# Moving the additive step of every RMSNorm from GpSimd to ScalarE in a one-layer hybrid decoder kernel

## The chip, the cores and the metric

The kernel runs on one core of one Trainium2 chip. The metric is the device time of one execution in microseconds (us). A core has five engines with queues of their own: TensorE (PE in the profile; its weight loads are PEld), VectorE (DVE), ScalarE (ACT), GpSimd (POOL) and SyncE (SP), which here only issues DMAs. Each queue runs in order; engines wait for one another through semaphores.

## The reference

One decoder layer over 512 tokens of 1024 channels, all in float32. The sub-layers matter here only for where the norms stand:

```
def rms_norm(x, g):
    y = x * rsqrt(mean(x * x, axis=-1) + 1e-6)
    return y * g

h = rms_norm(x, g_mix_pre);  u, q, k, v = split(h @ w_in)
y = concat[pool_mixer(u), moba_attention(q, k, v)] @ w_out
x = x + rms_norm(y, g_mix_post)
h = rms_norm(x, g_ffn_pre)
x = x + rms_norm(conv_ffn(h), g_ffn_post)
x = x + (p @ w_ple) * sigmoid(x @ w_ple_gate)
```

So there are four norms, each over 512 tokens.

## The kernel before

The 512 tokens are four tiles (t = 0 to 3) of 128 tokens, one token per partition. Every norm is done once per tile, so there are sixteen reciprocal roots, and, as one of the norms adds in two steps, twenty additions. Matmuls run in float32r; each operand is split into a high part (`h`) and a low part (`l`), and a product is three matmuls (`mm3`, L231 to L235). Weights arrive by SyncE's DMAs in two rotating `raw` buffers; ScalarE writes the high part `wh` (L146), VectorE the low part `wl` (L153), and when both halves of a chunk are split its `raw` buffer goes to the next load. How many splits run ahead is written into the program by `W.ahead(n)`; the order on each engine is the order of the code.

A norm of one tile is a chain over three engines. `mean_square` (L255) lets ScalarE square the tile and accumulate the mean square into a 128x1 column `ms`; the profile shows this as an ACTIVATE and an ACTIVATION_READ_ACCUMULATOR on L258. `rstd_of` (L261) then has GpSimd add a constant (L263) and raise to the power -0.5 (L264). VectorE multiplies the tile by the result.

- `first_norm(t)` (L341, names `msx`, `rx`, `hn`): the norm ahead of w_in. Its result is transposed on TensorE (`put_transposed`, L274) and split into `hT`; the value projections `v` stand between the tiles.
- The norm after w_out is over two halves of 512 channels that are finished at different times. The first half's mean square gets the constant at L635 on GpSimd (`s`, four columns); `second_norm(t)` (L641) takes the second half's mean square, and there `rstd_of` adds the column `s` in place of the constant (`ry`). VectorE updates the residual `x` (L646), and the norm ahead of the FFN follows at once (`msh`, `rh`, `h2n`, L649 to L653), then the transposes of that tile.
- `third_norm(t)` (L841, `msd`, `rd`): the norm after the FFN.

Of the kernel before, what the change touches and what calls it, by code (L numbers as in the profile page):

```python
# [17 lines left out]
F32 = mybir.dt.float32  # L18
F32R = mybir.dt.float32r
AF = mybir.ActivationFunctionType  # L20
ALU = mybir.AluOpType
# [3 lines left out]
P = 128  # L25
# [9 lines left out]
EPS = 1e-6  # L35
# [137 lines left out]
def hybrid_layer(ctx, tc, x, p, rel_bias, g_mix_pre, g_mix_post, g_ffn_pre, g_ffn_post, w_in, w_pool,  # L173
                 pool_scale, w_out, w_up, conv_w, conv_b, w_down, w_ple, w_ple_gate, onehot, out):
    nc = tc.nc
    act, dve, pool, pe, sp = nc.scalar, nc.vector, nc.gpsimd, nc.tensor, nc.sync

    const = ctx.enter_context(tc.tile_pool(name="const", bufs=1))
# [67 lines left out]
    pscale = cols[:, 4 * NF:]  # L246
    mhalf = const.tile([P, 1], F32, name="mhalf")
    pool.memset(mhalf, -0.5)

    def gains(pl, g, name):  # L250
        t = pl.tile([P, D], F32, name=name)
        pool.dma_start(t, bass.AP(tensor=g.tensor, offset=g.offset, ap=[[0, P], [1, D]]))
        return t

    def mean_square(src, junk, name):  # L255

        ms = small.tile([P, 1], F32, tag="ms", name=name)
        act.activation(junk, src, AF.Square, scale=D ** -0.5, accum_out=ms)  # L258
        return ms

    def rstd_of(ms, name, add=EPS):  # L261
        r = small.tile([P, 1], F32, tag="rstd", name=name)
        pool.tensor_scalar(r, ms, add, None, op0=ALU.add)  # L263
        pool.tensor_tensor(out=r, in0=r, in1=mhalf, op=ALU.pow)  # L264
        return r

# [74 lines left out]
    def first_norm(t):  # L341
        hn[t] = early.tile([P, D], F32, tag="hn", name=f"hn{t}", bufs=2)
        r = rstd_of(mean_square(xs[t], hn[t], f"msx{t}"), f"rx{t}")
        for c in range(2):
            part = slice(c * 512, (c + 1) * 512)
            dve.scalar_tensor_tensor(hn[t][:, part], xs[t][:, part], r, g_ps[c], op0=ALU.mult, op1=ALU.mult)
# [243 lines left out]
    def out_part(t, n, ks, first, last):  # L590
        if first:
            yb[t, n] = bank(f"y{t}_{n}", "mm" if t < 2 else "s")
        token_product(yb[t, n], t, wo, ks, first, last, y_stationary)
# [33 lines left out]
    for t in range(NT):  # L627
        out_part(t, 0, (3,) if t < 2 else (2, 7, 3), False, True)
        if t == NT - 1:
            wo = [W.take() for _ in range(4)]  # L630
            W.ahead(1)
        junk = op_.tile([P, D], F32, tag="hn", name=f"junk{t}", bufs=2)
        ms = mean_square(yb[t, 0], junk[:, :512], f"msy{t}_0")
        s = op_.tile([P, 1], F32, tag="s0", name=f"s0_{t}", bufs=NT)
        pool.tensor_scalar(s, ms, EPS, None, op0=ALU.add)  # L635
        s0.append(s)
        dve.tensor_mul(ya[t][:, :512], yb[t, 0], g_post[:, :512])
        if t < NT - 1:
            W.ahead(2)

    def second_norm(t, n=0):  # L641
        hn = op_.tile([P, D], F32, tag="hn", name=f"h2n{t}", bufs=2)
        ms = mean_square(yb[t, 1], hn[:, :512], f"msy{t}_1")
        dve.tensor_mul(ya[t][:, 512:], yb[t, 1], g_post[:, 512:])
        r = rstd_of(ms, f"ry{t}", s0[t])
        dve.scalar_tensor_tensor(X[t], ya[t], r, X[t], op0=ALU.mult, op1=ALU.add)  # L646
        if t:
            put_transposed(t - 1, h2[t - 1], "pt")
        ms = mean_square(X[t], hn, f"msh{t}")  # L649
        dve.tensor_mul(ya[t], X[t], g_pre)  # L650
        r = rstd_of(ms, f"rh{t}")
        W.ahead(n)
        dve.tensor_scalar_mul(hn, ya[t], r)  # L653
        h2.append(hn)
# [455 lines left out]
```

## Time and profile before

| | us |
|---|---|
| median of 3 runs | 592.13 (590.53 to 592.85) |
| the profiled execution | 590.47 |
| its span, first to last instruction | 588.6 |
| TensorE busy in the span | 580.1 |
| VectorE busy | 429.9 |
| ScalarE busy | 294.4 |
| GpSimd busy | 233.4 |

The busy times overlap, since the engines run side by side. The profiled execution lasts 1.87 us longer than its span, and it is a little faster than the fastest of the three timed runs. TensorE ran at its upper clock level nearly throughout: the mean granted clock is 0.998.

### The profile page before, as it was taken

The page shows a single profiled execution, that of the slowest core. Times are in us where ns is not written, and L with a number is a line of the kernel's source. Part 1 is how long each engine was busy: PE and PEld are TensorE (multiplying, and loading weights), DVE is VectorE, ACT ScalarE, POOL GpSimd, SP SyncE. Part 2 cuts the span into 40 slices and gives each one's busy share as a digit, 9 for nine tenths or more (in the row PEclk, how much of TensorE's full clock was granted, in tenths as well). Part 3 has the DMA queues.
Part 4 walks back from the last instruction along what each step waited for, and adds up shares of the span by engine and source line. Part 5 has one row for each costly group of instructions (what it writes and reads, how often), then busy time and mean ns, then how long its engine had stood idle before and what let it go on. Part 6 is the DMA issues. An engine that isn't in the chain of part 4 may idle for free.

```text
span 588.6 us, 7522 instructions
## 1 busy us (share of the span) xinstructions
PE 580.1 (99%) x2765; PEld 484.8 (82%) x2765; DVE 429.9 (73%) x560; ACT 294.4 (50%) x478; POOL 233.4 (40%) x236
## 2 busy tenths in 40 slices
PE   8999999999999999999999999999999999999996
PEld 6788888888879988888888888888888888888885
DVE  5625786888488668697854667967777785879985
ACT  6524665665455424334432434535465665757561
POOL 2200230066035389999604696574210000003920
PEclk9999999999999999999999999999999999999999
DMA  8779833624640988999935566858364575768563
GB/s 293 207 250 293 225 102 90 171 82 177 221 139 0 338 306 272 361 338 362 330 122 168 190 215 218 296 200 286 142 205 153 198 286 179 267 199 307 188 222 139
DMA packets 70237, 128.58 MB, mean 218 GB/s; under 512 B 4163, under 2 KB 37791, under 8 KB 68792
## 3 DMA queue, kind: packets, MB, share of 16 engines
q1 hardware_dynamic: 60472, 88.56, 46.9%
q0 software_dynamic: 9584, 39.41, 18.2%
q8 instruction: 22, 0.36, 0.2%
q10 hardware_dynamic: 144, 0.13, 0.1%
q14 instruction: 15, 0.12, 0.1%
HBM read 97.65 MB, written 26.76 MB: 211 GB/s over the span
## 4 chain that ended last, share of the span: by engine, by line
PE 91%; DMA 3%; DVE 2%; ACT 2%; issue 1%; SPq 1%; POOL 0%; DVEq 0%; ACTq 0%; POOLq 0%
PE gate L233 6%; PE valu L233 6%; PE gate L234 6%; PE valu L235 6%; PE gate L235 6%; PE valu L234 6%; PE d L233 6%; PE d L235 6%; PE d L234 6%; PE g L233 2%; PE g L235 2%; PE g L234 2%; PE s L464 2%; PE o L513 2%; DMA xa<-in_x 2%; PE pt L493 1%
## 5 line engine op out<-in xcount | busy, mean ns | idle before, releaser
L153 DVE TENSOR_TENSOR wl<-raw,wh 128x1024 fp32r<-128x1024 f32 (+1 forms) x118 | 161.7, 1378 | 25.5 <-ACT wh L146 25.2
L146 ACT CAST wh<-raw 128x1024 fp32r<-128x1024 f32 (+1 forms) x118 | 119.0, 1024 | 28.7 <-DMA raw<-in_w_up 13.2
L769 POOL TENSOR_TENSOR b<-b 128x512 f32<-128x512 f32 x60 | 96.6, 1621 | 12.1 <-DMA b<-in_w_down 9.6
L233 PE MATMUL gate<-hT,wl 128*128 128x512 f32 x160 | 62.3, 389 | 0.0
L234 PE MATMUL gate<-hT,wh 128*128 128x512 f32 x160 | 62.3, 389 | 0.0
L234 PE MATMUL valu<-hT,wh 128*128 128x512 f32 x160 | 62.2, 389 | 0.0
L235 PE MATMUL valu<-hT,wh 128*128 128x512 f32 x160 | 62.2, 389 | 0.0
L235 PE MATMUL gate<-hT,wh 128*128 128x512 f32 x160 | 62.2, 389 | 0.0
L233 PE MATMUL valu<-hT,wl 128*128 128x512 f32 x160 | 62.2, 389 | 0.0
L233 PE MATMUL d<-wh,ml 128*128 128x512 f32 x154 | 60.0, 390 | 0.1
L235 PE MATMUL d<-wh,mh 128*128 128x512 f32 x154 | 59.9, 389 | 0.0
L234 PE MATMUL d<-wl,mh 128*128 128x512 f32 x154 | 59.9, 389 | 0.0
L263 POOL TENSOR_SCALAR rd<-msd 128x1 f32<-128x1 f32 x4 | 1.7, 422 | 108.3 <-ACT M L258 108.3
L713 ACT ACTIVATE sq<-sq 128x512 f32<-128x512 f32 x22 | 13.9, 632 | 53.4 <-DVE sq L712 53.4
L701 ACT ACTIVATE c<-gate,cols 128x512 f32<-128x512 f32 x20 | 15.4, 772 | 48.4 <-PE gate L235 48.4
L534 POOL TENSOR_TENSOR u<-u 128x512 f32<-128x512 f32 x10 | 10.6, 1063 | 72.1 <-ACT u L530 71.6
L235 PEld LDWEIGHTS gate<-hT,wh 128*128 128x128 f32 x160 | 30.0, 188 | 6.3
L235 PEld LDWEIGHTS valu<-hT,wh 128*128 128x128 f32 x160 | 30.0, 188 | 6.3
L234 PEld LDWEIGHTS valu<-hT,wh 128*128 128x128 f32 x160 | 30.0, 188 | 6.2
L233 PEld LDWEIGHTS valu<-hT,wl 128*128 128x128 f32 x160 | 30.0, 188 | 6.2
L233 PEld LDWEIGHTS gate<-hT,wl 128*128 128x128 f32 x160 | 30.0, 188 | 6.2
L234 PEld LDWEIGHTS gate<-hT,wh 128*128 128x128 f32 x160 | 30.0, 188 | 6.2
(252 smaller groups left out, 1334.5 us busy)
## 6 DMA issues: line engine op xcount, KB each, us to landing
raw<-in_w_up SPq DMA_DIRECT2D x22, 1024.0 KB, 5.9
b<-in_w_down POOLq DMA_DIRECT2D x22, 512.0 KB, 7.1
tsum<-b POOLq DMA_DIRECT2D x11, 1024.0 KB, 5.4
raw<-tsum SPq DMA_DIRECT2D x20, 512.0 KB, 4.3
raw<-in_w_down SPq DMA_DIRECT2D x15, 512.0 KB, 4.5
raw<-in_w_in SPq DMA_DIRECT2D x12, 512.0 KB, 6.4
k<-qk SPq DMA_DIRECT2D x16, 256.0 KB, 4.8
raw<-in_w_out SPq DMA_DIRECT2D x4, 1024.0 KB, 5.3
```

The source lines that it names most:

```text
L146: self.nc.scalar.copy(pair[0], view)
L153: self.nc.vector.tensor_sub(pair[1], view, pair[0].bitcast(F32))
L233: pe.matmul(o, st[1], mv[0], start=first, stop=False, skip_group_check=more)
L234: pe.matmul(o, st[0], mv[1], start=False, stop=False, skip_group_check=more)
L235: pe.matmul(o, st[0], mv[0], start=False, stop=last, skip_group_check=more)
L464: pe.matmul(bk[b][:, c:c + n], q[:, i * P:n], k[:, a, :n], start=a == 1, stop=a == 0)
L493: pe.transpose(ps[:, c * P:(c + 1) * P], L[h][:, o:o + P], ident)
L513: pe.matmul(o, w, moving(PT[c], j), start=j == 0 and c == 0, stop=j == NT - 1 and c == 1)
L534: pool.tensor_tensor(out=nxt[:, 16:], in0=src[:, 16:], in1=src[:, 16 - (1 << lvl):16 + S - (1 << lvl)], op=ALU.add)
L701: act.activation(c0, pg, AF.Identity, bias=cw[:, 3, f:f + 1], scale=cw[:, 2, f:f + 1])
L713: act.activation(sq, sq, AF.Tanh, scale=GELU_A * GELU_C)
L769: pool.tensor_tensor(out=b[:, o, :], in0=b[:, i0, :], in1=b[:, i1, :], op=ALU.subtract)
```

## The change

All additions of the norms go from GpSimd to ScalarE. A column `eps` of 128x1 is filled once at the start; an Identity activation with a bias column adds it, or the column `s`, to the mean square. The power stays on GpSimd.

```
+    eps = const.tile([P, 1], F32, name="eps")
+    pool.memset(eps, EPS)
...
     def rstd_of(ms, name, add=EPS):
         r = small.tile([P, 1], F32, tag="rstd", name=name)
-        pool.tensor_scalar(r, ms, add, None, op0=ALU.add)
+        act.activation(r, ms, AF.Identity, bias=eps if add is EPS else add)
         pool.tensor_tensor(out=r, in0=r, in1=mhalf, op=ALU.pow)
         return r
...
         s = op_.tile([P, 1], F32, tag="s0", name=f"s0_{t}", bufs=NT)
-        pool.tensor_scalar(s, ms, EPS, None, op0=ALU.add)
+        act.activation(s, ms, AF.Identity, bias=eps)
         s0.append(s)
```

TensorE, VectorE and SyncE keep their order. ScalarE's queue gets 20 instructions, each right behind the squares it belongs to; the two table loads in it stay two. GpSimd's loses 20 and gets the one that fills `eps`.

ScalarE's queue from the last tile's first half (`msy3_0`) to the second tile's second half (`msy1_1`), before:

```order
L258 ACTIVATE junk3_1573,msy3_0_1574<-y3_0_1444 128x512
L238 CAST pT0_1487<-trp0_1604 128x512
L238 CAST pT0_1487<-trp1_1611 128x512
L146 CAST wh25_1618<-raw12_1524 128x1024
L258 ACTIVATE h2n0_1624,msy0_1_1625<-y0_1_1579 128x512
L258 ACTIVATE h2n0_1624,msh0_1632<-x0_1478 128x1024
L258 ACTIVATE h2n1_1677,msy1_1_1678<-y1_1_1639 128x512
```

And ScalarE's same stretch after the change (lines are two higher; `h2n0` and `msh0` belong to tile 0):

```order
L260 ACTIVATE junk3_1575,msy3_0_1576<-y3_0_1446 128x512
L637 ACTIVATE s0_3_1578<-msy3_0_1576,eps_84 128x1
L238 CAST pT0_1489<-trp0_1606 128x512
L238 CAST pT0_1489<-trp1_1613 128x512
L146 CAST wh25_1620<-raw12_1526 128x1024
L260 ACTIVATE h2n0_1626,msy0_1_1627<-y0_1_1581 128x512
L265 ACTIVATE ry0_1630<-msy0_1_1627,s0_0_1515 128x1
L260 ACTIVATE h2n0_1626,msh0_1634<-x0_1480 128x1024
L265 ACTIVATE rh0_1637<-msh0_1634,eps_84 128x1
L260 ACTIVATE h2n1_1679,msy1_1_1680<-y1_1_1641 128x512
```

Three additions (`s0_3`, `ry0`, `rh0`) now stand between these rows; the casts of `pT` and of `wh25` come behind the first of them.

GpSimd's queue over the same stretch, before:

```order
L635 TENSOR_SCALAR s0_2_1547<-msy2_0_1545 128x1
L635 TENSOR_SCALAR s0_3_1576<-msy3_0_1574 128x1
L263 TENSOR_SCALAR ry0_1628<-msy0_1_1625,s0_0_1513 128x1
L264 TENSOR_TENSOR ry0_1628<-ry0_1628,mhalf_82 128x1
L263 TENSOR_SCALAR rh0_1635<-msh0_1632 128x1
L264 TENSOR_TENSOR rh0_1635<-rh0_1635,mhalf_82 128x1
L263 TENSOR_SCALAR ry1_1681<-msy1_1_1678,s0_1_1532 128x1
```

And GpSimd's queue after the change, from the DMA ahead of these rows on:

```order
L624 DMA pin_1491<-in_p 128x4x256
L266 TENSOR_TENSOR ry0_1630<-ry0_1630,mhalf_82 128x1
L266 TENSOR_TENSOR rh0_1637<-rh0_1637,mhalf_82 128x1
L266 TENSOR_TENSOR ry1_1683<-ry1_1683,mhalf_82 128x1
L266 TENSOR_TENSOR rh1_1704<-rh1_1704,mhalf_82 128x1
```

Only the powers are left there.

## Rows read from the trace of the kernel before

**Rows 1.** The page: busy time of each engine.

```profile
PE 580.1 (99%) x2765; PEld 484.8 (82%) x2765; DVE 429.9 (73%) x560; ACT 294.4 (50%) x478; POOL 233.4 (40%) x236
```

**Rows 2.** Windows: length, busy PE, PEld, DVE, ACT, POOL, clock, DMA, GB/s.

```profile
0.00:2.00 2.00, 0.65 (x3) 0.65 (x4) 0.21 (x1) 1.27 (x1) 1.33 (x9) 1.00 0.01 2
...
12.00:20.00 8.00, 7.08 (x36) 4.95 (x35) 6.48 (x10) 6.24 (x12) 3.03 (x7) 1.00 1.10 329
...
172.00:175.00 3.00, 2.65 (x17) 2.10 (x16) 2.91 (x4) 1.43 (x3) 0.93 (x2) 1.00 0.02 6
175.00:200.00 25.00, 25.00 (x184) 23.63 (x183) 18.57 (x22) 12.23 (x21) 13.60 (x18) 1.00 0.31 107
...
510.00:545.00 35.00, 35.00 (x164) 29.13 (x163) 28.44 (x33) 23.63 (x37) 7.02 (x10) 1.00 0.72 244
...
580.00:588.60 8.60, 3.23 (x15) 2.34 (x13) 4.14 (x8) 1.26 (x3) 0.00 (x0) 0.88 0.32 122
```

**Rows 3.** Line L263 by tile: ns min/median/max, first and last start.

```profile
L263 POOL TENSOR_SCALAR ry<-msy,s x4: 292/690/1705, 166.5 to 183.8; 128x1 f32<-128x1 f32 x4
L263 POOL TENSOR_SCALAR rh<-msh x4: 216/993/1079, 170.9 to 188.8; 128x1 f32<-128x1 f32 x4
```

**Rows 4.** ScalarE's groups by shape: busy us, mean ns, idle before.

```profile
L473 ACT ACTIVATE L<-L,m 128x512 f32<-128x512 f32 x8 | 5.8, 724 | 7.0 <-DVE m L471 7.0
...
L473 ACT ACTIVATE L<-L,m 128x128 f32<-128x128 f32 x8 | 3.1, 387 | 0.0
...
L238 ACT ACT_TABLE_LOAD x1 | 1.3, 1283 | 0.7 <-PEq L1093 0.7
```

**Rows 5.** Timelines, GpSimd's and VectorE's, tile 3: start, duration, instruction.

```profile
189.94 1.39 POOL L264 TENSOR_TENSOR rh<-rh,mhalf 128x1 f32<-128x1 f32 x1
...
189.70 1.22 DVE L153 TENSOR_TENSOR wl<-raw,wh 128x1024 fp32r<-128x1024 f32 x1
```

**Rows 6.** Timelines of the first norm, tiles 1 and 2: POOL, DVE, ACT, PE.

```profile
15.73 0.81 POOL L263 TENSOR_SCALAR rx<-msx 128x1 f32<-128x1 f32 x1 [2.97 <-ACT hn L258]
...
14.11 2.36 DVE L153 TENSOR_TENSOR wl<-raw,wh 128x1024 fp32r<-128x1024 f32 x2
17.23 1.40 DVE L346 SCALAR_TENSOR_TENSOR hn<-xa,rx,g_pre 128x512 f32<-128x512 f32 x2 [0.76 <-POOL rx L264]
18.55 1.28 DVE L239 TENSOR_TENSOR hT<-tr,hT 128x512 fp32r<-128x512 f32 x2
...
15.55 1.06 ACT L238 CAST hT<-tr 128x512 fp32r<-128x512 f32 x2
...
19.29 0.66 PE L274 MATMUL tr<-ident,hn 128*128 128x128 f32 x4 [0.54 <-DVE hT L239]
```

**Rows 7.** The chain that ended last, around 157 us: start, us, what.

```profile
156.96 5.17 DMA raw<-in_w_up
```

**Rows 8.** Timelines of tile 0 behind w_out: ACT, POOL, DVE, PE.

```profile
162.21 1.05 ACT L146 CAST wh<-raw 128x1024 fp32r<-128x1024 f32 x1 [3.68 <-DMA raw<-in_w_up]
...
166.12 0.22 ACT L258 ACTIVATION_READ_ACCUMULATOR h2n<-y 128x1 f32 x1
...
166.51 1.09 POOL L263 TENSOR_SCALAR ry<-msy,s 128x1 f32<-128x1 f32 x1 [1.92 <-ACT h2n L258]
167.68 0.57 POOL L264 TENSOR_TENSOR ry<-ry,mhalf 128x1 f32<-128x1 f32 x1
...
166.23 1.22 DVE L153 TENSOR_TENSOR wl<-raw,wh 128x1024 fp32r<-128x1024 f32 x1
167.36 0.69 DVE L644 TENSOR_TENSOR ya<-y,g_mix_post 128x512 f32<-128x512 f32 x1
168.28 1.28 DVE L646 SCALAR_TENSOR_TENSOR x<-ya,ry,x 128x1024 f32<-128x1024 f32 x1 [0.24 <-POOL ry L264]
...
171.79 0.80 DVE L653 TENSOR_SCALAR h2n<-ya,rh 128x1024 f32<-128x1024 f32 x1 [0.97 <-POOL rh L264]
...
172.65 1.09 PE L274 MATMUL tr<-ident,h2n 128*128 128x128 f32 x8 [0.35 <-DVE h2n L653]
```

More of the change, by code (lines that the diff above doesn't have):

```diff
@@ L248, in hybrid_layer @@
     pool.memset(mhalf, -0.5)
+    eps = const.tile([P, 1], F32, name="eps")
+    pool.memset(eps, EPS)
     def gains(pl, g, name):
@@ L262, in rstd_of @@
         r = small.tile([P, 1], F32, tag="rstd", name=name)
-        pool.tensor_scalar(r, ms, add, None, op0=ALU.add)
+        act.activation(r, ms, AF.Identity, bias=eps if add is EPS else add)
         pool.tensor_tensor(out=r, in0=r, in1=mhalf, op=ALU.pow)
@@ L634, in hybrid_layer @@
         s = op_.tile([P, 1], F32, tag="s0", name=f"s0_{t}", bufs=NT)
-        pool.tensor_scalar(s, ms, EPS, None, op0=ALU.add)
+        act.activation(s, ms, AF.Identity, bias=eps)
         s0.append(s)
```

## The prediction

> **What bounds the kernel now.** The page's busy times come first: TensorE is busy for 580.1 us, 99% of the span, the next engine (VectorE) for 429.9 [rows 1]. So only idle time of TensorE can be won, and a step on another engine costs something only where TensorE comes to wait for it. The windows then say where TensorE is idle: 1.35 us at the start (2.00 - 0.65), 0.92 between 12 and 20 us, 0.35 between 172 and 175, and 5.37 after 580, where only the last sigmoid, product and store are left [rows 2]. Of the 8.5 idle (588.6 - 580.1) these make 8.0, and 0.5 lies elsewhere. The start is the building of the identity matrix, the end holds no norm. What a norm can be blamed for is thus at most 0.92 + 0.35 = 1.27 us. The remaining question is what the waits in those two places end on, and the timelines there answer it. At 19.29 TensorE waits 0.54 for VectorE's `hT`, which stands behind `hn`, which waits for GpSimd's `rx` [rows 6]. At 172.65 it waits 0.35 for `h2n`, which VectorE starts after waiting 0.97 for GpSimd's `rh` [rows 8].
>
> **What one addition costs on either engine.** Alone, the addition takes 0.22 on GpSimd (the minimum), but its median for `rh` is 0.99 and the longest `ry` took 1.71 [rows 3]. The long ones are waits for VectorE: the `ry` of tile 0 ends at 167.60, and the two-operand `wl` that ran meanwhile at 166.23 + 1.22 = 167.45 [rows 8]. The power waits in the same way: for tile 3 it ends at 189.94 + 1.39 = 191.33, which is 0.41 after that `wl` (189.70 + 1.22 = 190.92) [rows 5].
>
> ScalarE has no 128x1 ACTIVATE before. The exponentials with a bias column take 724 ns at 512 columns and 387 at 128 [rows 4]: (724 - 387) / 384 = 0.88 ns a column, so 387 - 128 x 0.88 = 0.27 is left at zero columns, and 0.28 at one. From both sides: the accumulator read of 128x1 takes 0.22 [rows 8], the 128-column exponential 0.39. The new instruction also waits for the accumulator read just ahead of it on its own engine, which no row shows. The nearest row is GpSimd's power behind its addition: 167.60 to 167.68, 0.08 [rows 8]. The bounds are 0 and 0.17 (accumulator read ends 166.34, GpSimd starts 166.51 [rows 8]). I take 0.08, so each addition pushes ScalarE's queue back by 0.08 + 0.28 = 0.36 (0.22 to 0.56).
>
> For the chain of one norm this gives two cases. Where VectorE is out of the way, 0.22 + 0.08 on GpSimd becomes 0.28 + 0.08 on ScalarE: 0.06 later (-0.08 to +0.26). Where VectorE holds GpSimd up, the addition now passes during the hold, and only the power waits. Before, the root came 0.15 + 0.08 + 0.57 = 0.80 after VectorE's instruction ended (tile 0, 167.45 to 168.25 [rows 8]); now it comes 0.41 after it [rows 5]: 0.39 earlier.
>
> **A rule weighed here.** What the rows show is that GpSimd's addition and its power both stretch to the end of a VectorE instruction, while no ScalarE row here does so. The Trainium skill ("SBUF — State Buffer", Who interferes with whom) says that a VectorE instruction with two SBUF inputs and a GpSimd instruction that reads SBUF exclude each other for a whole instruction, that whoever starts first wins, and that ScalarE never waits. The trace agrees on the first with the 191.33 against 190.92. By that rule a power that comes earlier can also hold VectorE up, which speaks against the change; that is the second rival.
>
> **The parts.**
> - *First norm, tiles 0, 1 and 3.* Zero. Tile 0's addition falls while ScalarE waits for the first weights; for the others VectorE and TensorE have other work between. Bounds -0.2 and +0.3 (one addition at its dear end).
> - *First norm, tile 2.* The addition stood at 15.73 for 0.81, held up by two `wl` that end at 14.11 + 2.36 = 16.47 [rows 6]. Now the power alone waits and ends at 16.47 + 0.41 = 16.88, so `hn` starts at 16.91 in place of 17.23: 0.32 earlier. `hT` follows it without a pause (18.55 to 18.23). The casts that `hT` needs move back from 15.55 by 0.36 and end near 16.97, still ahead of it. TensorE's wait of 0.54 at 19.29 shrinks by 0.32 [rows 6]. If the power meets the hold of the whole of VectorE's run as the addition did, nothing is won: bounds -0.54 and 0. I take -0.32.
> - *Norm after w_out and before the FFN, tile 0.* Here four additions add up on ScalarE. That of `s0_0` pushes back the split that frees a `raw` buffer, and with it the load issued at 156.96 [rows 7] for which ScalarE waits at 162.21 [rows 8]: +0.36. That of `s0_3` stands between this cast and `h2n`: +0.36. So the accumulator read ends at 166.34 + 0.72 = 167.06, the `ry` addition at 167.42, and the power could start at 167.5. VectorE's `wl` of 166.23 waits for a cast in the same queue; the instructions ahead of it cover half of the delay, and it ends near 167.81. The power ends 0.41 later, at 168.22, and the residual update follows `L644`, itself pushed to 168.35, in place of 168.28: +0.07. The `rh` addition is unhindered: +0.06. `h2n` and the transposes behind it come 0.13 later, and TensorE's wait grows from 0.35 to 0.48 [rows 8]. If the load's landing doesn't move and the `wl` isn't late, the hold alone ends sooner and TensorE gains up to 0.35; if nothing covers the 0.72 and both additions are dear, it loses 0.72 + 0.2 = 0.9. I take +0.13, near the rows of the same tile.
> - *Tiles 1 to 3 there.* Zero: TensorE is busy 25.00 of 25.00 between 175 and 200 [rows 2], so it does not wait for them, and additions that come 0.06 later or 0.39 earlier stay inside that cover. Queued behind each addition on ScalarE are the casts of `hT` and of `wh`, for which TensorE would wait if the cover were gone: up to 0.36 a tile, some 0.3 in all as a bound.
> - *Norm after the FFN.* Zero: TensorE is busy 35.00 of 35.00 between 510 and 545 [rows 2]. The four additions delay ScalarE's weight casts by 0.36 each, and those run ahead of TensorE by several splits; if that lead were gone they would cost 1.4 at most.
> - *GpSimd.* The fill of `eps` at the start stands ahead of two small loads that are used many us later; the twenty additions that go were never what GpSimd's later work waited for. Zero.
>
> Sum: -0.32 + 0.13 = -0.19 us on the profiled execution's 590.47 (span 588.6 and 1.87 outside it): 590.3. The median of the runs shown, 592.13, is 1.66 above that execution, so the same difference puts the median at 591.9. Runs of one kernel spread over 2.3 us, far more than the sum, and that governs the range.
>
> **Rivals.**
> - *Nothing is won.* The power takes over the whole wait of the addition at tile 2 (it is held for as long as before), and tile 0 loses its 0.13. For it: the 1.71 addition [rows 3] sat through more than one VectorE instruction. Against it: the power ends 0.41 after the hold, where addition and power needed 0.80. Time 592.13 + 0.1 = 592.2.
> - *The power gets in first and VectorE waits.* At tile 0 and tile 2 the power comes up to 0.3 earlier and may hold a two-operand instruction for its 0.57. Time 592.13 + 2 x 0.57 - 0.2 = 593.1. Against it: at 167.36 VectorE's next instruction had started 0.32 ahead of the power and neither was stretched [rows 8].
> - *The wait on its own engine is dear.* If ScalarE's addition with its wait costs about as much as its longest fixed instruction, the table load of 1.28 [rows 4], in place of 0.36, each costs 0.92 more. Tile 0's chain behind w_out meets four (`s0_0` through the load, `s0_3`, `ry`, `rh`): 4 x 0.92 = 3.7; the first norm's tiles 1 and 2 meet one each, 1.8. Time 591.9 + 5.5 = 597.4, slower. It decides from about 0.55 more per addition (6 x 0.55 - 0.2 = 3.1), that is from an addition of 0.9. Nothing in the profile speaks for it but that no ScalarE row there waits for the one right ahead; the hand-offs that rows show are 0.08 to 0.17.
> - *All of the wait goes.* The two places lose their whole 0.92 + 0.35: 592.13 - 1.27 = 590.9. It needs loads and the transposes' banks to come earlier too, which the change doesn't touch.
>
> The Trainium skill ("ScalarE: Activation LUTs", What ACT_TABLE_LOAD costs) puts a drain of some 1.38 us beside a table load; by that, if an ordinary wait had it, the dear rival would hold. No row here shows such a drain.
>
> **How the numbers follow.** A measurement of this kernel can tell about 0.5%, 2.96 us, from no change. The forecast (-0.2, likeliest at 591.9) has 0.58, nothing won 0.16, the power first 0.10, all of the wait 0.09, the dear wait 0.05, and 0.02 is left for what I don't see. All but the dear wait lie within 0.5%: same 0.92. Slower 0.05, for the dear wait and a slip in the spread. Faster 0.03: even the whole 1.27 isn't enough, so it takes luck of the runs as well. The terms' bounds add up to about -1.1 and +2.9, but not all ends can be met together; with the scatter of the runs the range is 589.8 to 593.8, and the dear wait is left out of it.
>
> **What would show it.** Twenty 128x1 ScalarE instructions of about 0.28, starting about 0.08 after the accumulator read; powers on GpSimd that end 0.41 after VectorE's instruction where they were held; TensorE's wait at 19.3 down to some 0.2, and that at 172.7 near 0.5; busy TensorE unchanged at 580 us. I am wrong if a ScalarE addition takes over 0.9 with its wait, if TensorE gets a new wait between 175 and 545 us, or if its idle time outside start and end moves by more than 1 us.

## The result and the profile after

The changed kernel takes 597.08 us (median of five runs, 595.84 to 598.14), against 592.13 for the kernel before in the same rounds (590.42 to 593.71). The ratio is 1.0088, 95% interval 1.0064 to 1.0112: slower by some 5 us, outside the predicted range of 589.8 to 593.8. The profiled execution took 595.84, with a span of 594.0, 5.4 more than before.

The page of after, the row that answers to [rows 1] (busy us, share of the span, instructions):

```profile
PE 580.9 (98%) x2765; PEld 484.9 (82%) x2765; DVE 429.2 (72%) x560; ACT 299.4 (50%) x498; POOL 221.8 (37%) x217
```

TensorE is busy 0.8 us longer than before and idle for 594.0 - 580.9 = 13.1 us in place of 8.5. So 4.6 of the 5.4 are waiting, and the question is where. TensorE's waits in after (what waits, for what: us in total, times, longest):

```profile
PE gate L233 <- DVE c L705: 3.5, 1, 3.5
PE s L466 <- issue: 1.9, 1, 1.9
...
PE tr L276 <- DVE hT L239: 0.4, 1, 0.4
```

The first row is new: the trace of before has no wait of the gate product. The second was 0.2 before. The windows of after (us, busy PE, PEld, DVE, ACT, POOL, clock, DMA share, GB/s) answer to [rows 2], and the fourth is a place at which no term of the prediction stood:

```profile
12.00:20.00 8.00, 7.38 (x38) 5.43 (x38) 6.66 (x9) 7.30 (x15) 1.91 (x4) 1.00 1.11 330
...
172.00:175.00 3.00, 2.99 (x18) 2.23 (x17) 1.99 (x4) 1.67 (x7) 1.40 (x2) 1.00 0.55 190
175.00:200.00 25.00, 25.00 (x179) 23.31 (x178) 20.05 (x23) 13.85 (x27) 9.76 (x13) 1.00 0.31 104
208.90:212.80 3.90, 0.45 (x4) 0.27 (x4) 2.89 (x4) 3.40 (x5) 3.51 (x6) 1.00 0.87 295
```

Two waits shrank: 0.92 to 0.62 between 12 and 20, and 0.35 to 0.01 between 172 and 175 (the second is gone in profiles without the change too, as the step on tile 0 below shows). Against these 0.64 stand the 3.45 near 209 and 1.7 more at the scores (`s`). Why TensorE stands still near 209 is told by the chain that ended last, in order of time (start, us, what):

```profile
190.03 0.30 ACT rh L265
190.33 0.95 ACT wh L146
...
191.30 1.24 DVE wl L153
...
192.55 16.17 DMA raw<-in_w_up
...
208.80 1.05 ACT wh L146
...
209.88 0.04 DVE wl L153
...
211.80 0.76 DVE c L705
212.56 0.14 issue
212.69 0.47 PE gate L233
```

Read it backwards. The gate product needs a bank that VectorE's `c` frees. `c` stands in VectorE's queue behind the `wl` of a weight split (209.88), and that waits for ScalarE's cast `wh` (208.80). The cast waits for a load of `w_up`, which SyncE issued at 192.55 and which took 16.17 us. It was issued when the split behind tile 3's norm ahead of the FFN was done, with the moved addition (190.03) in front of it.

The same load lay in before too, and took 6.3. The views of the transfers' issues, before first, then after (issue, operation, count, KB, us to landing):

```profile
raw<-in_w_up SPq DMA_DIRECT2D x1, 1024.0 KB, 6.3
```

```profile
raw<-in_w_up SPq DMA_DIRECT2D x1, 1024.0 KB, 16.2
```

What differs is who is ahead of whom. The timelines of tile 3's norm in before, ScalarE, GpSimd and SyncE (start, us, instruction; the power at 189.94 is in [rows 5]):

```profile
188.51 0.18 ACT L258 ACTIVATION_READ_ACCUMULATOR h2n<-x 128x1 f32 x1
188.60 1.03 ACT L146 CAST wh<-raw 128x1024 fp32r<-128x1024 f32 x1
...
191.29 2.54 POOL L689 DMA_DIRECT2D xd<-x  x4
...
190.94 13.77 SPq L118 DMA_DIRECT2D raw<-in_w_up  x3
```

And in after, ScalarE, GpSimd, VectorE and SyncE:

```profile
189.74 0.20 ACT L260 ACTIVATION_READ_ACCUMULATOR h2n<-x 128x1 f32 x1
190.03 0.30 ACT L265 ACTIVATE rh<-msh,eps 128x1 f32<-128x1 f32 x1
190.23 1.03 ACT L146 CAST wh<-raw 128x1024 fp32r<-128x1024 f32 x1
...
190.41 0.95 POOL L266 TENSOR_TENSOR rh<-rh,mhalf 128x1 f32<-128x1 f32 x1 [3.36 <-ACT rh L265]
...
191.31 2.52 POOL L691 DMA_DIRECT2D xd<-x  x4
...
191.30 1.22 DVE L153 TENSOR_TENSOR wl<-raw,wh 128x1024 fp32r<-128x1024 f32 x1 [0.35 <-ACT wh L146]
...
192.55 6.71 SPq L118 DMA_DIRECT2D raw<-in_w_up  x2
```

Behind tile 3's power GpSimd issues four stores of `x` (`xd`, 512 KB each) and then loads of `w_down`. Counted from the end of the accumulator read, the `w_up` load was issued 2.25 later in before (190.94 - 188.69) and 2.61 in after (192.55 - 189.94): the addition on ScalarE pushes it back by 0.36. The stores were issued 2.60 later in before (191.29 - 188.69) and 1.37 in after (191.31 - 189.94), 1.23 earlier: the power now starts before VectorE's `wl`, which held it in before, and gets done. So the load, 0.35 ahead of the first store, comes to be 1.24 behind it.

What that does to the transfers is in the queues' rows (queue, packets, MB, share of 16 engines; q1 holds SyncE's loads, q0 GpSimd's transfers). Before, 191 to 195 us:

```profile
q1 hardware_dynamic: 754, 0.77, 71.4%
```

After, 194 to 206 us:

```profile
q0 software_dynamic: 920, 3.36, 77.7%
q1 hardware_dynamic: 1027, 1.05, 25.0%
```

In before the load has the engines to itself, though the stores are issued from 191.29 on. In after the two queues go packet for packet (920 and 1027), but a packet of q0 carries 3.36 MB / 920 = 3.7 KB and one of the load 1.0 KB. The load gets a quarter of the engines, and its 1.05 MB takes the whole 12 us.

The Trainium skill ("DMA: Bandwidth & Descriptors", Queues, rings and completion order) says that each DMA engine takes turns between the queues for which it has work, packet by packet. The trace of after agrees, 920 to 1027. So does that of before between 202 and 206, 321 packets of q0 to 319 of q1. But before does not show it for the load in question: stores issued 0.35 behind it moved nothing between 191 and 195, where turns would have given them four fifths of the bytes (3.7 of 4.7 KB).

### The profile page after: what moved, and what is told of

Its sections match the earlier page's. It is cut to its first block, busy times and chain, and to the rows that moved or that the text cites. A ratio compares the mean times of both kernels' runs of the same rounds, so it can differ in the third digit from the quotient of the medians.

```text
span 594.0 us, 7513 instructions
## 1 busy us (share of the span) xinstructions
PE 580.9 (98%) x2765; PEld 484.9 (82%) x2765; DVE 429.2 (72%) x560; ACT 299.4 (50%) x498; POOL 221.8 (37%) x217
## 4 chain that ended last, share of the span: by engine, by line
PE 87%; DMA 7%; DVE 2%; ACT 2%; issue 1%; SPq 1%; POOL 0%; ACTq 0%; DVEq 0%
PE gate L233 6%; PE gate L234 6%; PE valu L234 6%; PE gate L235 6%; PE valu L235 6%; PE valu L233 6%; PE d L233 5%; PE d L234 5%; PE d L235 5%; DMA raw<-in_w_up 3%; PE y L235 3%; PE y L233 3%; PE y L234 2%; PE g L233 2%; PE g L234 2%; PE g L235 2%
## 5 line engine op out<-in xcount | busy, mean ns | idle before, releaser
L266 POOL TENSOR_TENSOR rd<-rd,mhalf 128x1 f32<-128x1 f32 x4 | 2.2, 551 | 110.4 <-ACT rd L265 110.4
```

## Experiments

The theory after the first comparison: the loss comes from the order of one load against GpSimd's stores, not from the additions as such. The rival: each of the twenty additions costs its own share on ScalarE, some 0.25 us. The kernels of this table tell them apart; each row holds the issue time of the `w_up` load less that of the first store of `x` (us), the load's time to landing, TensorE's wait for the gate product in the profile, and the ratio to the kernel before with its interval.

| kernel | load - store | landing | wait | ratio |
|---|---|---|---|---|
| before | -0.35 | 6.3 | none | 1 |
| after | +1.24 | 16.2 | 3.5 | 1.0088 [1.0064, 1.0112] |
| e1_first | -0.36 | 6.1 | none | 0.9992 [0.9977, 1.0007] |
| e2_second | +1.24 | 15.9 | 3.1 | 1.0102 [1.0075, 1.0129] |
| e3_third | -0.34 | 6.4 | none | 0.9996 [0.9981, 1.0012] |
| e4_rh3 | +1.16 | 16.3 | 3.8 | 1.0087 [1.0060, 1.0114] |
| a_ahead_first | -0.33 | 6.3 | none | 0.9998 [0.9981, 1.0014] |
| a_xd_sp | -0.42 | 6.6 | none | 1.0011 [0.9994, 1.0028] |
| a_xd_early | +3.63 (last store) | 5.1 | none | 1.0021 [1.0007, 1.0035] |
| b_delay | +0.85 | 7.3 | none | 1.0000 [0.9988, 1.0012] |
| b_delay2 | +1.05 | 16.1 | 3.8 | 1.0118 [1.0098, 1.0137] |
| a_fill | +1.24 | 16.0 | filled | 1.0073 [1.0056, 1.0089] |
| a_vb_ahead | -0.34 | 6.3 | none | 1.0011 [0.9997, 1.0026] |
| b_vb | -0.34 | 6.2 | none | 1.0005 [0.9993, 1.0017] |

### One part of the change at a time

Four kernels move only some additions to ScalarE; the others stay on GpSimd. The edit, against after, is this one, with another set of names in each; in e1_first, e3_third and e4_rh3 the column `s` (L637) goes back to GpSimd as well:

```
     def rstd_of(ms, name, add=EPS):
         r = small.tile([P, 1], F32, tag="rstd", name=name)
-        act.activation(r, ms, AF.Identity, bias=eps if add is EPS else add)
+        if name[:2] in ("rx",):
+            act.activation(r, ms, AF.Identity, bias=eps if add is EPS else add)
+        else:
+            pool.tensor_scalar(r, ms, add, None, op0=ALU.add)
```

**e1_first** moves the four of the first norm (`rx`).

> Only the first norm's four additions are on ScalarE, the other sixteen stay on GpSimd. Theory (order of transfers): of the two new waits of TensorE only the one near 60 us appears. There the pieces of k come late because TensorE runs 0.5 us earlier from 20 us on while the bias table's two transfers on GpSimd's queue end 0.9 later. TensorE's wait ahead of the scores is about 1.9 us in place of 0.24, nothing at 209, and the time is about 1.2 us above the kernel before. Rival (each ScalarE addition costs its own share of the 5 us): 4 of 20 additions, 1.0 us, spread over the first norm, with no long wait near 60.

Measured: 591.61 us (590.23 to 592.88), before 591.8. The wait at the scores came (1.6), the 1.2 us expected from it did not, and neither did the rival's 1.0.

**e2_second** moves the twelve of the norms after w_out and ahead of the FFN (`ry`, `rh` and the column `s`).

> Only the twelve additions behind w_out and ahead of the FFN are on ScalarE. Theory: the load of w_up issued after tile 3's split comes more than 0.5 us behind GpSimd's first store of xd, is served behind it and takes 14 us or more in place of 8; TensorE waits about 3.5 us near 207, and nothing new near 60. Time 3 to 4 us above before. Rival (each addition its own share): 12 of 20, 3.0 us, but as small waits at the transposes of the four tiles and no single long one.

Measured: 598.79 us (595.04 to 599.05). The whole loss is in this part. It is more than the 3 to 4 us expected, with the wait of 3.1 about as expected.

**e3_third** moves the four of the norm after the FFN (`rd`).

> Only the four additions of the norm behind the FFN are on ScalarE. Theory: no transfer changes its place, so the time is that of before within 0.3 us. Rival (each addition its own share): 1.0 us slower.

Measured: 591.63 us (590.55 to 593.0).

**e4_rh3** moves a single addition, tile 3's `rh` (the condition is `name in ("rh3",)`).

> A single addition, that of the last tile ahead of the FFN, is on ScalarE; nineteen stay on GpSimd. Theory: it alone swaps the w_up load and the stores of xd: the load is issued some 0.3 us later and the power ends earlier since it is not held by the split, so the stores come first; TensorE waits 2 to 3.5 us near 207. Time 2 to 3.5 us above before. Rival (each addition its own share): 0.25 us, not to be seen.

Measured: 597.64 us (594.98 to 599.06). One addition of twenty brings what all twenty bring, so the rival falls; but the loss is above the expected 2 to 3.5. The windows of this kernel (columns as above) show something more:

```profile
205.00:209.50 4.50, 4.50 (x39) 4.38 (x37) 0.00 (x0) 0.00 (x0) 3.96 (x4) 1.00 1.05 376
209.50:213.40 3.90, 0.09 (x1) 0.00 (x0) 2.75 (x4) 3.35 (x5) 3.51 (x6) 0.85 0.90 309
213.40:219.00 5.60, 5.57 (x13) 4.44 (x14) 5.01 (x4) 1.13 (x2) 4.84 (x4) 0.50 0.99 332
219.00:222.00 3.00, 3.00 (x14) 2.44 (x14) 2.61 (x2) 1.58 (x3) 2.90 (x5) 0.99 1.11 413
```

TensorE's granted clock falls while the engine stands still (0.85 over those 3.9 us) and is at 0.50, its lower level of 1.2 GHz, for the 5.6 us up to 219. There 13 matmuls pass in 5.57 us of work; at the 14 in 3.00 of the next row they would take 2.8, so the clock costs an estimated 2.8 us in this execution. The window from 214 to 217 in e2_second and then in b_delay2 (below) shows the same level, behind waits of 3.1 and 3.8:

```profile
214.00:217.00 3.00, 3.00 (x8) 2.31 (x7) 2.96 (x4) 0.00 (x0) 2.92 (x3) 0.50 0.91 345
214.00:217.00 3.00, 3.00 (x8) 2.32 (x8) 2.96 (x4) 0.00 (x0) 2.71 (x2) 0.50 1.01 376
```

The profile of after has a wait of 3.45, longer than that of e2_second, and its clock stays at 1.00. So the length of the wait alone does not tell whether the clock falls.

### The order of load and stores

**a_ahead_first** keeps all twenty additions on ScalarE and writes the split ahead of the last of them:

```
-        r = rstd_of(ms, f"rh{t}")
         W.ahead(n)
+        r = rstd_of(ms, f"rh{t}")
```

> All twenty additions stay on ScalarE; in the norm ahead of the FFN the split of the next w_up chunk is written ahead of the rh addition instead of behind it. Order theory (the kernel loses its time because the w_up load of tile 3 is handed over behind GpSimd's four stores of x): the load is issued near 191.0 to 191.5 us and the first store of x after it, near 192; the load lands within 9 us, TensorE has no wait of over 1 us near 209, time 592.2 (591 to 593.5), the granted clock near 0.998. Rival (each addition costs its own share on ScalarE): still twenty additions, 597.

Measured: 591.64 us (589.78 to 594.92), before 591.56. Its timelines, GpSimd and SyncE:

```profile
190.16 1.40 POOL L266 TENSOR_TENSOR rh<-rh,mhalf 128x1 f32<-128x1 f32 x1 [4.10 <-ACT rh L265]
191.51 2.53 POOL L691 DMA_DIRECT2D xd<-x  x4
...
191.18 14.06 SPq L118 DMA_DIRECT2D raw<-in_w_up  x3
```

The power is held again (1.40), the load is 0.33 ahead of the stores, and with the order the time is back.

**a_xd_sp** lets SyncE issue the stores, behind the load in its own queue:

```
     for t in range(NT):
-        pool.dma_start(xd[t], X[t])
+        sp.dma_start(xd[t], X[t])
```

> All twenty additions on ScalarE; the four stores of x after the FFN's norm are issued by SyncE, behind the w_up load in its queue, instead of by GpSimd. Order theory: the load is ahead of the stores by the queue's own order, it lands within 9 us of its issue and the wait near 209 is gone: 592.2 (591 to 593.5); the loads of the next chunks then stand behind the stores in SyncE's queue, which may cost up to 1. Rival (each addition costs its own share): 597.

Measured: 592.43 us (590.8 to 594.58). The loss is gone without touching any norm.

**a_xd_early** issues each tile's store right behind that tile's update; the loop behind the last norm goes:

```
         dve.scalar_tensor_tensor(X[t], ya[t], r, X[t], op0=ALU.mult, op1=ALU.add)
+        pool.dma_start(xd[t], X[t])
```

> All twenty additions on ScalarE; each tile's store of x is issued by GpSimd right behind that tile's update, so that three of four stores are out before the w_up load of tile 3 and only the last one can be ahead of it. Order theory: at most 0.5 MB stands against the load in place of 2 MB, so it lands in 8 to 11 us instead of 16 and the wait near 209 falls from 3.5 to under 0.5: 592.2 (591 to 593.5). If it is the presence of any store ahead that costs, not their sum: 597.

Measured: 592.9 us (590.57 to 594.09). The wait is gone; what the remaining 0.2% is was not followed up.

**b_delay** leaves every addition on GpSimd and puts one spare ScalarE instruction of the addition's form ahead of tile 3's cast:

```
         r = rstd_of(ms, f"rh{t}")
+        if t == NT - 1:
+            d = small.tile([P, 1], F32, tag="rstd", name="spare")
+            act.activation(d, ms, AF.Identity, bias=eps)
         W.ahead(n)
```

> All twenty additions on GpSimd as before, and one spare 128x1 ScalarE instruction between tile 3's squares and the cast behind them. Order theory: cast, split and load come 0.36 later (load near 191.3), but GpSimd's power is held by the same split and its stores of x move too (near 191.6), so the load stays ahead: same as before, 592 (591 to 593). Rival (a delay of ScalarE by one addition at this place is dear in itself): 597, as with the one addition moved.

Measured: 591.99 us (590.3 to 593.1). The time came out as expected, but not the way to it. The load did fall behind, by 0.85: with the cast later, GpSimd's power ran unheld, as in after. ScalarE's, GpSimd's and SyncE's timelines, and then the queues between 194.5 and 200:

```profile
190.08 0.19 ACT L260 ACTIVATION_READ_ACCUMULATOR h2n<-x 128x1 f32 x1
...
190.36 1.08 POOL L268 TENSOR_SCALAR rh<-msh 128x1 f32<-128x1 f32 x1 [2.65 <-ACT h2n L260]
191.52 0.56 POOL L269 TENSOR_TENSOR rh<-rh,mhalf 128x1 f32<-128x1 f32 x1
192.03 2.66 POOL L697 DMA_DIRECT2D xd<-x  x4
...
192.88 13.37 SPq L118 DMA_DIRECT2D raw<-in_w_up  x3
```

```profile
q1 hardware_dynamic: 1040, 1.05, 67.8%
q0 software_dynamic: 110, 0.38, 20.4%
```

The first store goes, and then the load passes at two thirds of the engines, with the other three stores waiting. So being behind one store is cheap, and the simple form of the theory (behind means slow) was too simple.

This kernel also takes the change's 1.59 (from -0.35 to +1.24) apart. Counted from the end of the accumulator read (190.27), the load is issued after 2.61, as in after, so its being 0.36 later is not the loss. The first store is issued after 1.76, against 2.60 in before and 1.37 in after: 0.84 of its 1.23 come from ScalarE's delay alone, which lets the power in ahead of `wl` (0.56 in place of 1.39), and the other 0.39 from the addition that is gone from GpSimd (0.31 in e4_rh3, which differs from this kernel in nothing else). In the change only these 0.39 take the order to +1.24.

**b_delay2** has two such spare instructions.

```
+            for i in range(2):
+                d = small.tile([P, 1], F32, tag="rstd", name=f"spare{i}")
+                act.activation(d, ms, AF.Identity, bias=eps)
```

> All twenty additions on GpSimd, and two spare 128x1 ScalarE instructions between tile 3's squares and the cast behind them, where the run with one spare put the load 0.85 behind GpSimd's first store of x and cost nothing. Order theory: the load is now some 1.2 behind the first store, as with the change (1.24), so it is handed over behind the second store too, lands after about 16 us and TensorE waits 3 to 4 us near 209: 597 (595.5 to 598.5), with no addition on ScalarE. Rival (what counts is that the addition is on ScalarE, or that GpSimd's power comes earlier): 592, as with one spare.

Measured: 598.63 us (596.86 to 599.57), before 590.92, with all additions on GpSimd; just above the expected range, though the load is only 1.05 behind in place of 1.2. GpSimd's and SyncE's timelines:

```profile
190.58 0.56 POOL L269 TENSOR_TENSOR rh<-rh,mhalf 128x1 f32<-128x1 f32 x1
191.08 2.34 POOL L698 DMA_DIRECT2D xd<-x  x4
...
192.13 6.27 SPq L118 DMA_DIRECT2D raw<-in_w_up  x2
```

Four stores in 2.34 put the second at 191.08 + 0.59 = 191.67, so the load is 0.46 behind the second store; in b_delay it was 0.18 behind it (192.88 - 192.03 - 2.66 / 4). There the load passes, here it doesn't. The whole loss thus comes without any addition on ScalarE, from the order alone, and the point at which it turns lies between 0.85 and 1.05 behind the first store. What in the queues decides there, no row shows.

### What the clock has in it

**a_fill** is after with sixteen spare matmuls ahead of the gate product that waits:

```
+    ps = bank("fill", "pt")
+    for i in range(16):
+        pe.matmul(ps, h_stationary(0, 0)[0], h_moving(0)[0], start=True, stop=True)
```

> The change as it is, and sixteen spare matmuls of 128x512 on TensorE (16 x 0.23 = 3.7 us) ahead of the gate product that waits near 209, so that TensorE works through the wait instead of idling. If part of the 5 us is the clock that falls after the idle stretch: the granted clock is 0.998 or 0.999 in every run and the time is 595.5 (594.5 to 596.5), some 1.5 below the change's 597.1, though more work is done. If the clock has no part in it: 597 or a little more, and runs at 0.995 as before.

Measured: 595.61 us (594.13 to 596.73). The timeline of TensorE, and the windows of this kernel:

```profile
209.62 3.82 PE L796 MATMUL fill<-hT 128*128 128x512 f32 x16
```

```profile
208.90:212.80 3.90, 3.90 (x22) 3.36 (x21) 2.51 (x3) 3.34 (x4) 3.52 (x5) 1.00 0.94 314
212.80:219.00 6.20, 6.20 (x29) 5.12 (x28) 5.47 (x6) 1.47 (x3) 5.43 (x5) 1.00 0.98 327
```

The load is as late as in after, TensorE works through the wait, and the clock stays at 1.00 where e4_rh3 had 0.50. With 3.8 us of spare work the kernel is not slower than after. That fits a share of the clock in the loss, about 1 us (the ratios differ by 0.0015, 0.9 us). The executions of after point the same way: the profiled one has a mean granted clock of 0.999 and takes 595.84, the other four have 0.995 and take 596.95 to 598.14; of the six of a_fill one has 0.995. But the intervals overlap, and the kernel before, without the wait, spreads over 3.3 us too, so the size for the change isn't settled. That the clock can fall there is shown by the profiles of e4_rh3, e2_second and b_delay2.

### The scores' wait

**a_vb_ahead** is a_ahead_first with the copies of the bias table moved ahead of `first_norm(2)`, and **b_vb** is before with the same move:

```
+    for c in range(2):
+        act.mul(vb[:, c * VW // 2:(c + 1) * VW // 2], vb_ps[c][:H, :VW // 2], -1.0)
+    pool.memset(vb[:, S:], MASKED)
     first_norm(2)
```

> The change with the split written ahead of the rh addition, and the copies of the bias table (vb) moved ahead of the norm of tile 2, so that its transfers start earlier. If the wait of the first scores (0.2 to 2.6 us in the profiles so far) ends on the transfers that follow that table: it falls to about 0.2 and the time is 591.0 (589.8 to 592). If it ends on something else (the scatter of the run's own start): 591.6, as without it.

> All additions on GpSimd as before, with the copies of the bias table moved ahead of the norm of tile 2. If the scores' wait ends on the transfers behind that table: 591.0 (590 to 592), with a smaller spread between runs; otherwise 591.8, as before.

Measured: 592.13 us (590.4 to 593.52) and 591.55 (590.07 to 593.42), before 590.92. Both miss. In the profile of a_vb_ahead the scores don't wait, and its span of 591.5 is long all the same; that of b_vb has a wait of 1.9 with every addition on GpSimd. So this wait moves between 0 and 2.6 us from profile to profile, with and without the change, and no run ties it to the time. No version found here beats the kernel before.

## Why the prediction was wrong, step by step

- *One addition on ScalarE.* Right. The group of the four `rh` in after (ns min/median/max):

```profile
L265 ACT ACTIVATE rh<-msh,eps x4: 294/294/296, 172.3 to 190.0; 128x1 f32<-128x1 f32 x4
```

  0.294 against 0.28, and for tile 3 it starts 0.09 behind the accumulator read (190.03 - 189.94) against 0.08; elsewhere it is 0.03 to 0.09. The cast behind it moves by 0.38 against 0.36.
- *The power ends 0.41 after VectorE's instruction.* Right, in place after place: 191.36 against the end of `ya` at 190.95 for tile 3.
- *First norm, tiles 1 and 2.* Right for VectorE: `hn` of tile 2 starts at 16.73 in place of 17.23 [rows 6]. Of these 0.50, 0.18 are an earlier end of `wl` (13.94 + 2.35 = 16.29 for 16.47) and 0.32 the shorter way from there, as predicted. For TensorE the sum is near, 0.30 less idle time for 0.32, but not its parts: tile 2's wait shrinks from 0.54 to 0.35 only, and tile 1, which was put at zero, loses a wait of 0.17. Tile 1 in before, tile 2 in after:

```profile
13.69 1.29 PE L274 MATMUL tr<-ident,hn 128*128 128x128 f32 x8 [0.17 <-DVE hn L346]
...
18.79 0.66 PE L276 MATMUL tr<-ident,hn 128*128 128x128 f32 x4 [0.35 <-DVE hT L239]
```

  So the sum fits by luck. In e1_first it is 0.35; in profiles where this norm comes some 2 us later it is hardly there (idle between 12 and 24: 0.77 in b_delay with the additions on GpSimd, 0.72 in a_fill with them on ScalarE).
- *Tile 0 behind w_out.* The chain was right, what TensorE makes of it was not. From the cast behind the load to `h2n` it takes 9.39 in after (163.90 to 173.29) against 9.58 in before [rows 8]; the prediction's terms (+0.13 in all, +0.36 of it up to the load) give 9.35. Predicted was +0.13 of waiting; in after TensorE has 0.01 idle between 172 and 175 and 25.00 of 25.00 busy behind it, so the wait of 0.35 is gone. But it is gone in e1_first and b_delay too, where these additions are on GpSimd and the chain takes 9.59; e1_first:

```profile
160.00:177.00 17.00, 17.00 (x83) 13.82 (x82) 12.96 (x16) 8.20 (x16) 4.11 (x8) 1.00 0.53 176
```

  So these 0.34 are no gain of the change as far as the runs show.
- *The norm after the FFN, and the first norm's tiles 0 and 3.* Right as far as times show: e1_first and e3_third are the same as before.
- *Tiles 1 to 3.* This step failed: "TensorE is busy 25.00 of 25.00 between 175 and 200, so it does not wait for them". It was busy there in after too, 25.00 of 25.00. But the casts that stand behind tile 3's addition end a split, the split frees a buffer, and the cast of what is loaded there runs 16 us later (208.80), with the gate product behind it. The step counted what TensorE would wait for at once, and not the load that SyncE issues behind the split, though the same path had been followed for tile 0's load at 156.96 [rows 7].
- *GpSimd.* This step failed with it: the additions that go "were never what GpSimd's later work waited for. Zero." They were, in part. The power of tile 3 got in ahead of the split that had held it for 1.39 [rows 5], and the four stores behind it came 1.23 earlier against the chain: 0.84 by ScalarE's delay, 0.39 by the addition gone from GpSimd, as b_delay shows. The second part is what took the load from a harmless +0.85 to +1.24. The step counted an earlier GpSimd as harmless, and did not ask what it issues next and what that runs into.
- *The rivals.* The dear wait gave 597.4, near the measured 597.1, but its mechanism is refuted by the 0.294 and the 0.09: its number came out by chance. The other rivals stayed within 1.3 us of before. The one with the power in first was half right: at tile 3 it came first, but VectorE did not wait for it (`wl` starts at 191.30, its cast ends at 191.26). None held a transfer that loses its place.

The prediction named what would prove it wrong: a new wait of TensorE between 175 and 545, or over 1 us of idle time more. Both came. The account of the profile is 3.45 at the gate product, 1.7 at the scores and -0.64 at the two shrunken waits, 4.5 of the 4.6 us of new idle time; the scores' part is scatter of a run, as b_vb shows. The medians differ by 5.0, and the wait alone takes 3.1 to 3.8 of it; what lies above that fits the clock, as far as a_fill and the mean clocks show it, and is otherwise open.

## What to carry to other kernels

When an instruction leaves a queue, look at the next DMAs behind it there, and ask against which transfers of other queues they now race: an earlier store can cost more than a later instruction. A chain that hands over a buffer has to be followed to the use of its next load, past any stretch in which the busy engine hides it. Where some tenths of a microsecond decide the order of two transfers, write it into the program (the split ahead of the addition, or both transfers in one queue).

## What the runs showed of the hardware

Two queues that shared the engines did so packet for packet: in after, loads of 1.0 KB a packet got 25.0% beside 77.7% for packets of 3.7 KB, and 1 MB took 16.2 us in place of 6.3. Which queue is first matters more than this sharing: with a load that was 0.35 ahead of the four stores, or 0.85 behind the first, the stores not yet begun stood back until it was nearly through; from 1.05 to 1.24 behind, the load shared with the stores and with what followed them. What decides between the two is not shown. The granted clock of TensorE fell to 0.50 around idle stretches of 3.1 and 3.8 us in three profiles (for 5.6 us in e4_rh3), and stayed at 1.00 with one of 3.45 us in a fourth. A power on GpSimd that VectorE's two-operand instruction held up ended 0.41 after it (191.36 for 190.95), while ScalarE's addition took 0.294 to 0.296 in every place.
